# First stage of a one-layer attention kernel: whole-bank casts, projections in sweeps, written order

## The chip, the cores and the metric

The kernel runs on one core of a Trainium2 chip. The metric is device time in microseconds (us); lower is better. A core has a matrix engine (TensorE, PE in the profile; its weight loads are PEld), three engines for elementwise work (VectorE, DVE; ScalarE, ACT; GpSimd, POOL) and a sync engine (SyncE, SP) that issues nearly all DMA transfers here. Each engine runs its own instructions in their order; semaphores order them between engines.

## The reference

One layer with sparse attention (three branches: compressed, selected, window) over x of 512 tokens by 1024. The part that the change touches is the norm, the first two projections and what is made of them:

```python
u = rms_norm(h, pre_norm_gain[layer])
q, kv, g, z = split_cols(h @ w_in, [NSA_WIDTH, 6 * NSA_KV_WIDTH, 3 * H, 3 * NSA_WIDTH])   # h is u here
k_c, v_c, k_s, v_s, k_w, v_w = [a.reshape(B, S, G, dh) for a in jnp.split(kv, 6, axis=-1)]
kc = compress_kv(k_c, k_pos, k_w1, k_w2)
vc = compress_kv(v_c, v_pos, v_w1, v_w2)

def compress_kv(kv, pos, w1, w2):
    idx = jnp.arange(n_cmp)[:, None] * CMP_STRIDE + jnp.arange(CMP_BLOCK)[None, :]
    blocks = kv[:, idx] + pos[None, None, :, None, :]
    ...
    return jax.nn.silu(flat @ w1) @ w2
```

A table of 32 x 16 relative position biases is spread to bias rows for the softmaxes (t5_bucket). The rest (three attentions, gates, output projection, second norm) is the same in both kernels.

## The kernel before, in words

Every float32 product is made of three matmuls on halves of the numbers: a high part (a cast, wh or uh) and a low part (the number less its high part, wl or ul); the products are high x high, low x high, high x low (`pass3`). PSUM has eight banks of 128 x 512 in four pairs, named after what they are for: ps_pj, ps_s, ps_t, ps_o.

The first stage goes through four token tiles of 128. For each, ACT sums the squares (L306), POOL makes r, the inverse root (L86, L90), DVE scales two halves of 512 columns (L316) and PE transposes them, four 128 x 128 blocks into a bank (L321). From the bank ACT casts the high part uh and DVE subtracts for the low part ul, two k tiles, or 256 columns, at a time (L327, L328). Weights come in tiles of 512 rows by 256 columns (wr, one or two DMAs on SP, L103); the cast to wh and the subtraction to wl are ACT's and POOL's for even tiles and DVE's for odd ones (`split_ahead`, L113 to L118).

The k-compressed projection p_kc (tiles 0 and 1, one k half each) runs in two halves of the tokens, matmuls of 256 columns (L247 to L249); the second two token tiles are prepared while the first half runs. Then `tables` spreads the bias table: four matmuls to toep (L344, L345), 16 little ones of 33 x 16 to cb (L351, L352), copies by DVE, and DMAs on SP to DRAM and back (toepd, cmpb, bias, cbs). The v-compressed projection p_vc follows (tiles 2 and 3, matmuls of 512 columns, in two ps_s banks), with DVE's block sums (`blocks`, eight instructions on L407 for k and eight for v) beside it; then the v projection p_v (L480 to L482; tiles 4, 6, 8 and 10 of the weights), between which the compression's own products run (L425 to L427; tiles 5, 7, 9, 11).

The program is given to a scheduler, which sets the order on each engine by its own estimates, except for instructions that are put in written order by `keep_in_program_order`; before, these are only the sums of squares and r. `issue_after(i)` keeps what is written under it behind instruction i.

## Time and profile before

| what | value |
|---|---|
| time, median of 3 runs | 467.64 us (465.06 to 467.78) |
| profiled execution | 466.85 us, its span 465.0 us |
| mean granted clock of PE | 0.993 |
| busy: PE, PEld, DVE, ACT, POOL | 450.9, 375.3, 330.6, 274.3, 184.7 us |
| PE waits in total | 465.0 - 450.9 = 14.1 us |
| first projection matmul, first v-projection matmul | 10.24 us, 41.94 us |

A granted clock of 1.00 is 2.4 GHz and 0.50 is 1.2 GHz. Times within the profile count from the start of the span; the profiled execution's time is 1.85 us over the span. In the rows an entry reads: start, duration, engine, line, operation, out<-in by the program's names, and in brackets the idle time before it with what ended that. Matmuls are pipelined, so two of them overlap: their distance is the difference of their starts.

### The profile page before, as it was taken

What the parts mean: (1) busy time and instruction counts of PE and PEld (TensorE: products, weight loads), DVE (VectorE), ACT (ScalarE), POOL (GpSimd) and SP (SyncE); (2) the same over time, 40 slices, a digit from 0 to 9 for tenths busy, and PEclk for the clock granted to TensorE, in tenths of its full rate; (3) what the DMA queues carried; (4) which work ended last, traced back from release to release, by engine and by line L of the source; (5) the groups of instructions that cost most, each with busy time, mean ns of one, the idle gap of its engine ahead of it and who ended that gap; (6) DMA issues with size and microseconds to landing.
All of it is one profiled execution on the core that took longest, in us unless ns stands there. A gap on an engine that the chain in (4) does not pass through costs nothing.

```text
span 465.0 us, 6924 instructions
## 1 busy us (share of the span) xinstructions
PE 450.9 (97%) x2330; PEld 375.3 (81%) x2330; DVE 330.6 (71%) x801; ACT 274.3 (59%) x642; POOL 184.7 (40%) x185
## 2 busy tenths in 40 slices
PE   5999999999999999999999999999999999999994
PEld 4797888878888878888888788888878888888883
DVE  6869844851766888768769776885896667567685
ACT  5712232542766577767846867666776666467541
POOL 4424544242223453342463525245343342448212
PEclk9989999999999999999999999999999999999998
DMA  8489275263111321511132332024051211214113
GB/s 300 142 82 280 77 216 162 66 206 90 47 45 48 112 59 34 182 45 47 45 90 70 88 94 71 21 57 132 19 180 45 92 45 47 91 43 140 47 45 135
DMA packets 45501, 44.63 MB, mean 96 GB/s; under 512 B 7751, under 2 KB 38471, under 8 KB 45466
## 3 DMA queue, kind: packets, MB, share of 16 engines
q1 hardware_dynamic: 44424, 44.00, 31.9%
q8 instruction: 18, 0.29, 0.3%
q10 hardware_dynamic: 1042, 0.20, 0.2%
q14 instruction: 17, 0.14, 0.1%
HBM read 41.99 MB, written 2.20 MB: 95 GB/s over the span
## 4 chain that ended last, share of the span: by engine, by line
PE 89%; DVE 4%; ACT 3%; issue 2%; POOL 1%; DVEq 0%; POOLq 0%; ACTq 0%
PE ps_pj L146 11%; PE ps_pj L148 11%; PE ps_pj L147 11%; PE ps_s L591 9%; PE ps_t L681 7%; PE ps_o L715 4%; PE ps_o L714 4%; PE ps_pj L834 3%; PE ps_pj L835 3%; PE ps_pj L836 3%; PE ps_s L247 2%; PE ps_s L248 2%; PE ps_s L249 2%; PE ps_pj L247 2%; PE ps_pj L248 1%
## 5 line engine op out<-in xcount | busy, mean ns | idle before, releaser
L118 POOL TENSOR_TENSOR wl<-wr,wh 128x512 fp32r<-128x512 f32 x94 | 123.0, 1328 | 138.6 <-ACT wh L113 122.2
L146 PE MATMUL ps_pj<-uh,wh 128*128 128x512 f32 x240 | 99.0, 412 | 0.0
L148 PE MATMUL ps_pj<-ul,wh 128*128 128x512 f32 x240 | 94.2, 393 | 0.0
L147 PE MATMUL ps_pj<-uh,wl 128*128 128x512 f32 x240 | 94.2, 392 | 0.0
L604 ACT ACTIVATE p<-p,nm 128x512 f32<-128x512 f32 (+3 forms) x128 | 71.6, 560 | 24.3 <-DVE nm L603 23.5
L685 DVE TENSOR_TENSOR ptl<-ps_t,pth 128x512 fp32r<-128x512 f32 x80 | 55.0, 688 | 28.2 <-ACT pth L684 27.7
L113 ACT CAST wh<-wr 128x1024 fp32r<-128x1024 f32 x47 | 49.2, 1047 | 43.5 <-DMA wr<-in_nsa_w_in_dram 20.1
L591 PE MATMUL ps_s<-kd,q 128*128 128x512 f32 (+5 forms) x256 | 63.9, 336 | 0.7 <-DVE zs L699 0.6
L684 ACT CAST pth<-ps_t 128x512 fp32r<-128x512 f32 x80 | 46.4, 580 | 29.3 <-PE ps_t L681 28.7
L148 PEld LDWEIGHTS ps_pj<-ul,wh 128*128 128x128 f32 x240 | 45.1, 188 | 10.1
L591 PEld LDWEIGHTS ps_s<-kd,q 128*128 128x128 f32 x256 | 43.9, 189 | 9.0 <-DVE zs L699 1.2
L146 PEld LDWEIGHTS ps_pj<-uh,wh 128*128 128x128 f32 x240 | 45.2, 188 | 6.1
L147 PEld LDWEIGHTS ps_pj<-uh,wl 128*128 128x128 f32 x240 | 45.3, 189 | 5.8
L603 DVE CUSTOM_DVE_ANT_0 p<-ps_s,bias 128x128 f32<-128x128 f32 (+3 forms) x80 | 34.6, 447 | 20.7 <-PE ps_s L591 20.5
L681 PE MATMUL ps_t<-ident,p 128*128 128x128 f32 x320 | 48.4, 272 | 0.0
L681 PEld LDWEIGHTS ps_t<-ident,p 128*128 128x128 f32 x320 | 39.7, 140 | 9.4
L714 PE MATMUL ps_o<-pth,vt 128*128 128x512 f32 x80 | 33.7, 421 | 0.0
L603 DVE CUSTOM_DVE_ANT_1 p<-ps_s,bias 128x256 f32<-128x256 f32 (+2 forms) x48 | 26.3, 555 | 9.3 <-PE ps_s L591 8.6
L728 POOL TENSOR_TENSOR y<-otmp,zs 128x256 f32<-128x256 f32 x16 | 12.3, 771 | 51.5 <-DVE otmp L725 51.5
L715 PE MATMUL ps_o<-ptl,vt 128*128 128x512 f32 x80 | 32.3, 404 | 0.0
L730 POOL TENSOR_TENSOR otmp<-otmp,zs 128x256 f32<-128x256 f32 x15 | 11.1, 741 | 37.9 <-DVE otmp L725 37.9
L569 ACT ACTIVATE zs<-ps_pj 128x512 f32<-128x512 f32 x22 | 13.1, 596 | 19.4 <-PE ps_pj L148 19.3
(268 smaller groups left out, 895.6 us busy)
## 6 DMA issues: line engine op xcount, KB each, us to landing
wr<-in_nsa_w_in_dram SPq DMA_DIRECT2D x36, 512.0 KB
wr<-in_nsa_w_in_dram SPq DMA_DIRECT2D x16, 256.0 KB
bias<-toepd SPq DMA_DIRECT2D x16, 256.0 KB
wr<-in_nsa_w_out_dram SPq DMA_DIRECT2D x8, 512.0 KB
xt<-in_x_dram SPq DMA_DIRECT2D x4, 512.0 KB
wr<-in_nsa_cmp_k_w_dram SPq DMA_DIRECT2D x4, 512.0 KB
wr<-in_nsa_cmp_v_w_dram SPq DMA_DIRECT2D x4, 512.0 KB
xr<-in_x_dram SPq DMA_DIRECT2D x8, 256.0 KB
```

The costliest lines, as they stand in the source:

```text
L113: A.copy(h[:, 0:kn], raw[:, 0:kn])
L118: el.tensor_tensor(l[:, ks], raw[:, ks], h[:, ks].bitcast(F32), op=ALU.subtract)
L146: T.matmul(p, a, rh, start=k == 0, stop=False)
L147: T.matmul(p, b, rh, start=False, stop=False)
L148: T.matmul(p, a, rl, start=False, stop=k == KT - 1)
L591: T.matmul(po, qs[h][:, qt * 128:(qt + 1) * 128], kds[h // R][:, i, c0:c0 + n], start=i == 0, stop=i == 1)
L603: V.tensor_tensor_reduce(pd, src, bi, 1.0, BIG, ALU.add, ALU.min, st["nm"][:, hh:hh + 1])
L604: A.activation(po, po, AF.Exp, bias=st["nm"][:, hh:hh + 1], scale=-1.0, accum_out=st["rs"][:, hh:hh + 1])
L681: T.transpose(tp[:, hh * 128:(hh + 1) * 128], st["p"][hh][:, c:c + 128], ident)
L685: V.tensor_tensor(pl, tp, ph.bitcast(F32), op=ALU.subtract)
L714: T.matmul(acc, v, ph, start=j == 0, stop=False)
L715: T.matmul(acc, v, pl, start=False, stop=j == qt)
```

## The change

Everything in the first stage is put in written order (`put`). The u tiles are two of [128, 4, 512] for each part instead of four of [128, 2, 512], so that one ACT cast and one DVE subtraction take a whole bank of 512 columns (`high`, `low`). The projections run in sweeps (`sweep`): for one weight tile and one half of the tokens first all eight wh x uh, then eight wh x ul, then eight wl x uh. The v-compressed projection goes to ps_o banks, which two matmuls with a row of zeros open (`open_`); its first k half is swept by token halves among those of p_kc. The sum of squares of tile 2 moves from ACT to DVE (`rms(2, True)`). A third weight tile is loaded and split early. Odd weight tiles are split by ACT and POOL (tiles 1 to 3) or ACT and DVE, where before DVE did both. `load_pos`, the k blocks and `load_w2` are written earlier, `tables` later, behind the sweeps. Buffers with the tag "u" later in the program (y3, og, w3) get the new size.

```diff
-    uh = [keep.tile([128, 2, S], F32R, name=f"uh{i}", tag="u", bufs=8) for i in range(4)]
-    ul = [keep.tile([128, 2, S], F32R, name=f"ul{i}", tag="u", bufs=8) for i in range(4)]
+    uh = [keep.tile([128, 4, S], F32R, name=f"uh{i}", tag="u", bufs=4) for i in range(2)]
+    ul = [keep.tile([128, 4, S], F32R, name=f"ul{i}", tag="u", bufs=4) for i in range(2)]
...
-            tiles.append(split_raw(raws[i], 4, *((V, V) if i % 2 else (A, P))))
+            tiles.append(split_raw(raws[i], 4, *((A, V) if i % 2 and i > 3 else (A, P))))
...
+        zrow = a1.tile([1, 128], F32R, name="zrow")
+        V.memset(zrow.bitcast(F32), 0.0)
...
+        load_ahead(2)
...
-        def rms(t):
...
+        def rms(t, vec=False):
...
+            if vec:
+                put(V.tensor_tensor_reduce(sq, xs[t], xs[t], 1.0 / D, 0.0, ALU.mult, ALU.add, ss))
+            else:
+                put(A.activation(sq, xs[t], AF.Square, scale=1.0 / 32, accum_out=ss))
+            rs_[t] = a1.tile([128, 1], F32, name="r", bufs=4)
+            rstd(rs_[t], ss)
+
+        def scale(t, kq):
+            xt = xs[t][:, kq * 512:(kq + 1) * 512]
+            put(V.scalar_tensor_tensor(xt, xt, rs_[t], gain[kq], op0=ALU.mult, op1=ALU.mult))
+
+        def turn_(t, kq, home):
+            xt = xs[t][:, kq * 512:(kq + 1) * 512]
+            p = pt_[t, kq] = home()
+            for j in range(4):
+                put(T.transpose(p[:, j * 128:(j + 1) * 128], xt[:, j * 128:(j + 1) * 128], ident))
+
+        def norm(t, kq, home):
+            scale(t, kq)
+            turn_(t, kq, home)
...
+        def high(t, kq):
+            put(A.copy(*part(uh, t, kq)))
+
+        def low(t, kq):
+            d, p = part(ul, t, kq)
+            i = put(V.tensor_tensor(d, p, part(uh, t, kq)[0].bitcast(F32), op=ALU.subtract))
+            behind[:] = [i.ins]
+
+        def split_first(n):
+            h = wp.tile([128, 4, 256], F32R, name="wh", tag="wh", bufs=3)
+            l = wp.tile([128, 4, 256], F32R, name="wl", tag="wl", bufs=3)
+            put(A.copy(h, raws[n]))
+            tiles.append((h, l))
+
+            def rest(i):
+                ks = slice(i * 2, i * 2 + 2)
+                put(P.tensor_tensor(l[:, ks], raws[n][:, ks], h[:, ks].bitcast(F32), op=ALU.subtract))
+            return rest
+
+        def open_(ps_):
+            for p in ps_:
+                put(T.matmul(p, zrow, gh[:, 0:S], start=True, stop=False))
+
+        def sweep(n, ps_, kq, hs, opened=False):
+            h, l = tiles[n]
+            for w, u in ((h, uh), (h, ul), (l, uh)):
+                for kk in range(4):
+                    for m, p in enumerate(ps_):
+                        put(T.matmul(p[:, hs], w[:, kk, m * 128:(m + 1) * 128], u[kq][:, kk, hs],
+                                     start=not opened and kq == 0 and w is h and u is uh and kk == 0,
+                                     stop=kq == 1 and w is l and kk == 3))
+                yield
...
+        h0, h1 = slice(0, 256), slice(256, 512)
         rms(0)
         rms(1)
-        prep(0)
-        split_ahead(0)
-        prep(1)
-        split_ahead(1)
-        rms(2)
+        norm(0, 0, tb)
+        high(0, 0)
+        norm(0, 1, tb)
+        w0 = split_first(0)
+        w0(0)
+        w0(1)
+        norm(1, 0, ob)
+        low(0, 0)
+        high(1, 0)
+        norm(1, 1, ob)
+        low(1, 0)
+        p_kc = [pj(), pj()]
+        run(sweep(0, p_kc, 0, h0))
+        high(0, 1)
+        high(1, 1)
+        low(0, 1)
+        low(1, 1)
+        w1 = split_first(1)
+        w1(0)
+        rms(2, True)
+        w1(1)
         rms(3)
-        p_kc = [pj(), pj()]
-        for hh in range(2):
-            hs = slice(hh * 256, (hh + 1) * 256)
-            for k in range(KT):
-                if hh == 0 and k in (3, 5):
-                    prep(2 if k == 3 else 3)
-                h, l = tiles[k // 4]
-                for m in range(2):
-                    ms = slice(m * 128, m * 128 + 128)
-                    pass3(p_kc[m][:, hs], h[:, k % 4, ms], l[:, k % 4, ms], uh[k // 2][:, k % 2, hs],
-                          ul[k // 2][:, k % 2, hs], k == 0, k == KT - 1)
-            if hh == 0:
-                tables()
+        w2 = split_first(2)
+        w2(0)
+        w2(1)
+        s1 = sweep(1, p_kc, 1, h0)
+        next(s1)
+        next(s1)
+        norm(2, 0, tb)
+        high(2, 0)
+        run(s1)
+        norm(2, 1, tb)
+        high(2, 1)
+        scale(3, 0)
+        low(2, 0)
+        low(2, 1)
+        p_vc = [ob(), ob()]
+        open_(p_vc)
+        s2 = sweep(2, p_vc, 0, h0, True)
+        next(s2)
+        turn_(3, 0, tb)
+        high(3, 0)
+        scale(3, 1)
+        next(s2)
+        turn_(3, 1, tb)
+        high(3, 1)
+        low(3, 0)
+        low(3, 1)
+        run(s2)
+        run(sweep(0, p_kc, 0, h1))
+        with tc.issue_after(behind[0]):
+            kpt = load_pos("k")
+            vpt = load_pos("v")
+        run(sweep(1, p_kc, 1, h1))
+        kb = blocks(p_kc, kpt)
+        run(sweep(2, p_vc, 0, h1, True))
+        with tc.issue_after(behind[0]):
+            tables()
...
-        kpt = load_pos("k")
-        vpt = load_pos("v")
-        kb = blocks(p_kc, kpt)
-        p_vc = [sb(), sb()]
-        half_t(2, 0, p_vc)
+        with tc.issue_after(behind[0]):
+            kw2h, kw2l = load_w2("k", 2)
+            vw2h, vw2l = load_w2("v", 1)
+        kb = block_split(kb)
         half_t(3, 1, p_vc)
-        vb = blocks(p_vc, vpt)
-        kw2h, kw2l = load_w2("k", 2)
-        vw2h, vw2l = load_w2("v", 1)
+        vb = block_split(blocks(p_vc, vpt))
...
-                yhl[g] = [keep.tile([128, 2, S], F32R, name=f"y3{i}", tag="u", bufs=8) for i in range(2)]
+                t = keep.tile([128, 2, 2, S], F32R, name="y3", tag="u", bufs=4)
+                yhl[g] = [t[:, i] for i in range(2)]
...
-        og = [keep.tile([128, D], F32, name="og", tag="u", bufs=8) for _ in range(NT)]
+        og = [t[:, i] for t in [keep.tile([128, 2, D], F32, name="og", tag="u", bufs=4) for _ in range(2)] for i in range(2)]
...
-        w3 = [wo_tile(3, 0, [keep.tile([128, 4, 256], F32R, name="w3", tag="u", bufs=8) for _ in range(2)]),
+        wt = keep.tile([128, 2, 4, 256], F32R, name="w3", tag="u", bufs=4)
+        w3 = [wo_tile(3, 0, [wt[:, i] for i in range(2)]),
```

On PE, `tables` moves. Before, its matmuls stand within the first and second token half of p_kc (ps_pj), ahead of most of the second half; uh_80 and uh_81 are high parts, ul_84 a low part.

```order
L321 MATMUL ps_t<-ident,xt 128x128 x4
L344 MATMUL ps_s<-hsr,nth 16x512
L345 MATMUL ps_s<-hsr,ntl 16x512
L247 MATMUL ps_pj<-uh_80,wh 128x256
L321 MATMUL ps_o<-ident,xt 128x128 x4
L344 MATMUL ps_s<-hsr,nth 16x128
L345 MATMUL ps_s<-hsr,ntl 16x128
L248 MATMUL ps_pj<-uh_80,wl 128x256
```

In the changed kernel the same place is this: the last sweep over ps_o (p_vc, tile 2), the matmuls for toep, and then p_vc's second k half with ten matmuls ahead of the first of the 16 little ones (L405, L406).

```order
L379 MATMUL ps_o<-uh_80,wl 128x256 x8
L398 MATMUL ps_s<-hsr,nth 16x512
L399 MATMUL ps_s<-hsr,ntl 16x512
L398 MATMUL ps_s<-hsr,nth 16x128
L399 MATMUL ps_s<-hsr,ntl 16x128
L247 MATMUL ps_o<-uh_81,wh 128x512
L248 MATMUL ps_o<-uh_81,wl 128x512
L249 MATMUL ps_o<-ul_83,wh 128x512
```

The little matmuls moved behind all sweeps, into the projection of 512 columns; 14 of its 24 matmuls follow them.

On DVE, the block sums of k and the copies out of the tables' banks changed places. Before:

```order
L346 COPY toep<-ps_s 16x128
L353 COPY cb<-ps_s 128x8x4x4
L399 TENSOR_TENSOR kw2l<-w2k,kw2h 128x2x64
L398 CAST vw2h<-w2v 128x128
L399 TENSOR_TENSOR vw2l<-w2v,vw2h 128x128
L115 CAST wh<-wr 128x1024
L118 TENSOR_TENSOR wl<-wr,wh 128x512 x2
L463 TENSOR_TENSOR wgs<-wgr,wgs 128x8x48
L390 COPY ptk<-ps_t 128x32
L390 COPY ptv<-ps_t 128x32
L407 TENSOR_TENSOR blk<-ps_pj,ptk 64x16x31 x8
```

Now:

```order
L266 COPY ptk<-ps_t 128x32
L266 COPY ptv<-ps_t 128x32
L274 TENSOR_TENSOR blk<-ps_pj,ptk 64x16x31 x8
L400 COPY toep<-ps_s 16x512
L400 COPY toep<-ps_s 16x128
L118 TENSOR_TENSOR wl<-wr,wh 128x512 x2
L407 COPY cb<-ps_s 128x8x4x4
```

The copies stand behind the eight block sums, and the two wl halves of tile 5 stand between those of toep and that of cb.

On SP the DMAs of the tables stand between other weights. Before (the rows of two 128x2x256 parts are the two halves of tile 4, first, and of tile 6, last; the row named cmp_k_w is tile 5):

```order
L103 DMA wr<-in_nsa_w_in_dram 128x2x256 x2
L103 DMA wr<-in_nsa_cmp_k_w_dram 128x4x256
L347 DMA toepd<-toep 16x640
L356 DMA cmpb<-cb 128x8x4 x4
L163 DMA bias<-toepd 128x512 x4
L168 DMA cbs<-cmpb 128x1x128 x4
L103 DMA wr<-in_nsa_w_in_dram 128x2x256 x2
```

Now (tile 6 in two halves and tile 7 come first; the 128x2x256 part alone ahead of cmpb is the first half of tile 8, the one behind cbs its second half):

```order
L103 DMA wr<-in_nsa_w_in_dram 128x2x256 x2
L103 DMA wr<-in_nsa_cmp_k_w_dram 128x4x256
L401 DMA toepd<-toep 16x640
L103 DMA wr<-in_nsa_w_in_dram 128x2x256
L410 DMA cmpb<-cb 128x8x4 x4
L163 DMA bias<-toepd 128x512 x4
L168 DMA cbs<-cmpb 128x1x128 x4
L103 DMA wr<-in_nsa_w_in_dram 128x2x256
L103 DMA wr<-in_nsa_cmp_k_w_dram 128x4x256
```

The tables' DMAs stood ahead of tile 6 and now stand inside tile 8. From the first matmul of the v projection on, the instructions of PE are the same in the same order to the end.

## Rows read from the trace of the kernel before

**Rows 1.** The page, part 1: busy time, share of the span and instructions.
```profile
PE 450.9 (97%) x2330; PEld 375.3 (81%) x2330; DVE 330.6 (71%) x801; ACT 274.3 (59%) x642; POOL 184.7 (40%) x185
```

**Rows 2.** Waits of PE, whole span: what waited for what, total, times, longest.
```profile
PE ps_o L321 <- DVE xt L316: 0.4, 1, 0.4
PE ps_o L427 <- DVE wl L118: 0.4, 1, 0.4
```

**Rows 3.** Timeline of PE, 6 to 12 us: start, duration, what, idle before.
```profile
6.96 1.12 PE L321 MATMUL ps_t<-ident,xt 128*128 128x128 f32 x4 [1.92 <-DVE xt L316]
...
10.24 0.58 PE L247 MATMUL ps_pj<-uh,wh 128*128 128x256 f32 x1 [0.46 <-ACT uh L327]
...
11.04 0.28 PE L248 MATMUL ps_pj<-uh,wl 128*128 128x256 f32 x1
11.16 0.60 PE L321 MATMUL ps_t<-ident,xt 128*128 128x128 f32 x4
```

**Rows 4.** Timeline of PE, 18 to 29 us.
```profile
19.16 0.63 PE L321 MATMUL ps_t<-ident,xt 128*128 128x128 f32 x4 [0.57 <-issue]
...
24.64 0.58 PE L247 MATMUL ps_pj<-uh,wh 128*128 128x256 f32 x1
...
28.17 0.28 PE L248 MATMUL ps_pj<-uh,wl 128*128 128x256 f32 x1
...
29.00 0.28 PE L249 MATMUL ps_pj<-ul,wh 128*128 128x256 f32 x1
```

**Rows 5.** Busy time by stretch: PE, PEld, DVE, ACT, POOL, PEclk, DMA share, GB/s.
```profile
25.00:28.00 3.00, 3.00 (x15) 3.00 (x15) 1.11 (x5) 0.00 (x0) 0.35 (x1) 0.50 0.89 104
```

**Rows 6.** Timeline of PE, 41 to 58 us.
```profile
41.71 0.39 PE L249 MATMUL ps_s<-ul,wh 128*128 128x512 f32 x1
41.94 0.39 PE L480 MATMUL ps_pj<-wh,uh 128*128 128x512 f32 x1
...
49.63 0.40 PE L480 MATMUL ps_pj<-wh,uh 128*128 128x512 f32 x1
...
56.52 0.40 PE L480 MATMUL ps_pj<-wh,uh 128*128 128x512 f32 x1
```

**Rows 7.** Timeline of SP's DMA queue, 0 to 62 us: start and duration of the issues.
```profile
37.63 1.03 SPq L103 DMA_DIRECT2D wr<-in_nsa_w_in_dram  x2
...
55.70 0.88 SPq L103 DMA_DIRECT2D wr<-in_nsa_w_in_dram  x2
```

**Rows 8.** Timeline of ACT, 36 to 66 us.
```profile
43.46 1.05 ACT L113 CAST wh<-wr 128x1024 fp32r<-128x1024 f32 x1 [4.65 <-DMA wr<-in_nsa_w_in_dram]
...
59.37 1.05 ACT L113 CAST wh<-wr 128x1024 fp32r<-128x1024 f32 x1 [8.47 <-DMA wr<-in_nsa_w_in_dram]
```

**Rows 9.** Timeline of DVE, 0 to 56 us.
```profile
6.15 2.18 DVE L316 SCALAR_TENSOR_TENSOR xt<-xt,r,ps_s 128x512 f32<-128x512 f32 x3 [1.96 <-POOL r L90]
...
24.75 0.29 DVE L353 COPY cb<-ps_s 128x128 f32<-128x128 f32 x1 [1.33 <-PE ps_s L352]
...
28.34 1.29 DVE L118 TENSOR_TENSOR wl<-wr,wh 128x512 fp32r<-128x512 f32 x2
...
31.15 5.49 DVE L407 TENSOR_TENSOR blk<-ps_pj,ptk 64x496 f32<-64x496 f32 x8
...
52.20 3.47 DVE L118 TENSOR_TENSOR wl<-wr,wh 128x512 fp32r<-128x512 f32 x2
```

**Rows 10.** Timeline of POOL, 0 to 66 us.
```profile
8.30 2.50 POOL L118 TENSOR_TENSOR wl<-wr,wh 128x512 fp32r<-128x512 f32 x2 [0.75 <-ACT wh L113]
...
15.10 0.57 POOL L90 TENSOR_TENSOR r<-r,nhalf 128x1 f32<-128x1 f32 x1
...
51.71 3.41 POOL L118 TENSOR_TENSOR wl<-wr,wh 128x512 fp32r<-128x512 f32 x2
```

**Rows 11.** The page, part 5: costliest groups, busy and mean ns, idle before.
```profile
L685 DVE TENSOR_TENSOR ptl<-ps_t,pth 128x512 fp32r<-128x512 f32 x80 | 55.0, 688 | 28.2 <-ACT pth L684 27.7
...
L684 ACT CAST pth<-ps_t 128x512 fp32r<-128x512 f32 x80 | 46.4, 580 | 29.3 <-PE ps_t L681 28.7
```

More of the change, by code (lines that the diff above doesn't have):

```diff
@@ L256, in half_t, with load_pos, blocks @@
                 ms = slice(m * 128, m * 128 + 128)
-                pass3(p, h[:, kk, ms], l[:, kk, ms], uh[k // 2][:, k % 2, :], ul[k // 2][:, k % 2, :],
+                pass3(p, h[:, kk, ms], l[:, kk, ms], uh[k // 4][:, k % 4, :], ul[k // 4][:, k % 4, :],
                       k == 0, k == KT - 1)
+    def load_pos(nm):
+        pr = small[nm, "p"]
+        V.tensor_copy(pr[:, 1], pr[:, 0])
+        p = tb()
+        T.transpose(p[:, :32], pr.rearrange("p a b -> p (a b)"), ident[:32, :32])
+        pt = sm.tile([128, 32], F32, name="pt" + nm)
+        V.tensor_copy(pt, p[:, :32])
+        return pt
+    def blocks(banks, pt):
+        blk = keep.tile([128, 16, G, NCMP], F32, name="blk", tag="kd", bufs=4)
+        for m, p in enumerate(banks):
+            for gp in range(2):
+                for lp in range(2):
+                    V.tensor_tensor(
+                        blk[lp * 64:lp * 64 + 64, :, 2 * m + gp, :],
+                        view(p[gp * 64:gp * 64 + 64, :], lp, [[2, 16], [16, NCMP]]),
+                        view(pt[gp * 64:gp * 64 + 64, :], lp, [[2, 16], [0, NCMP]]), op=ALU.add)
+        return blk
     with tc.tile_pool(name="a1", bufs=1) as a1:
```

55 lines of the change are left out of this document (9 added, 46 removed).

## The prediction

> **What bounds the kernel now.** I read the page's busy shares first: TensorE (PE) is busy for 450.9 of 465.0 us, no other engine for more than 71% [rows 1]. So at most 14.1 us could be won by taking PE's waits away, and nearly all else of a gain has to come from less PE work or a higher clock. The waits of PE come next. About 9 us of the 14.1 lie before the first projection matmul (first rows of [rows 3]): input, norm and transposes, which the change leaves in place. Behind it the first stage has few, such as one of 0.57 us before a transpose [rows 4], one of 0.4 and one of 0.5 on the input chain [rows 2, 3]. Then the clock: in 25 to 28 us the granted clock is 0.50, the 1.2 GHz level [rows 5]. The same row has 15 matmuls of 256 columns in 3.00 us, one in 0.20; afterwards seven distances between such matmuls, 28.17 to 29.00, make 0.83, or 0.119 each [rows 4]. What PE did just ahead of the fall were the 16 little matmuls of the tables, up to 24.64 [rows 4]. From 24.64 to 28.17 stand 16 matmuls, which take 3.53 instead of 16 x 0.119 = 1.90: the low clock costs some 1.6 us.
>
> PE's order is the same in both kernels from the first matmul of the v projection to the end, and so is that of the other engines from about there. So the question is when PE reaches that matmul, which I call T: 41.94 before [rows 6]; and whether something that PE wants later is late.
>
> **The change part by part.** The sum goes by differences to T = 41.94.
>
> *Start of the sweeps, +0.86.* Before, the first projection matmul starts at 10.24 between transposes. Now all 16 transposes of two token tiles stand ahead. The third scaling ends at 6.15 + 2.18 = 8.33 [rows 9]; the first bank is transposed at 6.96 + 1.12 = 8.08 [rows 3]. Its high cast takes 0.58 and its low part 0.69, as the 128x512 forms do that read a bank elsewhere [rows 11]: 8.70 and 9.44. The fourth scaling stands behind that on VectorE (DVE): 9.44 + 0.73 (a third of 2.18) = 10.2; its transposes take some 0.9, as the first bank's do (1.12 with its tail [rows 3]): 11.1 instead of 10.24. Whole-bank casts save ScalarE (ACT) and DVE one fixed cost per pair; both have idle time here, so that is worth nothing on the path. The first three distances of the projection, 10.24 to 11.04, make 0.80 before [rows 3], where at the higher level 3 x 0.119 = 0.36 would do. I take it that this slow start now falls on the transposes: -0.44. If it doesn't, this term is 0.
>
> *PE's work, +0.05.* Four transposes fewer stand behind the start (16 for 20; 0.63 for four [rows 4]): -0.63. Two matmuls that open banks with zeros, 512 columns each at the distance 41.71 to 41.94 of 0.23 [rows 6]: +0.46. Half of the v-compressed projection runs in 48 matmuls of 256 columns at 0.119 instead of 24 of 512 at 0.228: +0.24. All else is only moved.
>
> *Waits that go, -0.98.* The 0.57 and the 0.41 in front of transposes [rows 2, 4] go, as written order leaves 24 matmuls of a sweep between a scaling and the next transpose.
>
> *A wait that comes before token tile 2, +0.13 to +0.98.* The sum of squares of tile 2 moves from ACT to DVE, as one 128x1024 instruction with both inputs in SBUF, at about 12.7; behind it come GpSimd's (POOL) two small steps of r, and these are queued behind a wl half. No row has this instruction. DVE work of that kind beside POOL tensor operations is slow in both: two wl halves on DVE take 1.29 alone (at 28.34 [rows 9]) and 3.47 beside POOL's two, which take 3.41 [rows 9, 10]. With no delay the sum, some 1.3 by these, ends at 14.0, the wl half of 1.25 [rows 10] beside it at 14.4; r's two steps take 0.8 (the second 0.57 [rows 10]), so r is there at 15.2 and the scaled half at 15.95. PE is ready at 11.1 + 40 x 0.119 = 15.86: it loses 0.13 with the handing over. With the wl half waiting for the sum it runs from 14.0 to 15.2, r comes at 16.0, the half at 16.8: 0.98. I take 0.98, because those rows are the nearest. [...]
>
> *The tables, +0.6.* The 16 little matmuls now stand inside the second half of the v-compressed projection, ten matmuls behind the four of toep. They reuse a bank whose copy (toep) stands on DVE behind eight block sums, 5.49 us [rows 9]. These start with the end of the k projection; PE has 24 x 0.119 + 0.6 + 10 x 0.228 = 5.7 us of work meanwhile, and the copies add about 0.9: PE waits some 0.6.
>
> *The low clock, 0, or -1.6 if it stays away.* The same little matmuls follow, now with an idle 0.6 in front. What PE did ahead of the fall is there again, so I count on it: 0. Dense sweeps in front speak for the other end, -1.6.
>
> *T.* 41.94 + 0.86 - 0.44 + 0.05 - 0.98 + 0.98 + 0.6 = 43.0 with both bad ends; 40.6 with both good ones (-0.85, -1.6).
>
> *What follows T: the weights of tile 8, 0 to +2.5.* On the SP queue the tables' DMAs stood ahead of tile 6 and stand now between the two halves of tile 8. Before, from the end of the cb copy, 25.04 [rows 9], it took to 37.63 until the next weights were issued behind cmpb, bias and cbs [rows 7], and these were cast at 43.46, with ACT idle for 4.65 on the DMA [rows 8]: 18.4 after the copy. PE wanted them at 49.63 [rows 6], so nobody saw it. Now PE wants tile 8 at T + 14.6 (56.52 less 41.94 [rows 6]), its low half 0.46 later. The cb copy ends 14 matmuls x 0.228 = 3.2 before T, or 4.8 before it at the low clock. By 18.4 and the casts (1.05 [rows 8], and 1.25 for POOL's first half) the low half is there at T + 17.5, 2.5 late (0.9 with the low clock). By the load of 55.70, cast at 59.37 [rows 7, 8], the time behind the issue is 3.7 and the low half comes at T + 15.4: 0.3 late, or none. Less traffic competes than before, so I take the middle, 1.4, and 0.5 with the low clock.
>
> *Costed at nothing:* the third weight tile loaded early (DMA, long before its sweep), odd tiles' high casts on ACT instead of DVE (ACT idles 4.65 before one of these casts [rows 8]; without that cover 1.05 each), fewer and larger buffers at the end (the same bytes released together), the memset. The wait for a wl of DVE at 91.89, 0.4 [rows 2], may go, as DVE loses work: 0 to -0.4. I take -0.4.
>
> **Sum.** 43.0 - 41.94 = +1.06, +0.5 for tile 8, -0.4: +1.2 with both bad ends. The clock holding gives 1.06 - 1.6 + 1.4 - 0.4 = +0.5 (T = 41.4), and no delay of tile 2 takes 0.85 off either. These four lie from -0.4 to +1.2. I take +0.75, the upper half, since the low clock is likelier than not: 466.85 + 0.75 = 467.6. The profiled execution is 466.85 and the median 467.64 (465.06 to 467.78), 0.8 above it, well within what runs differ by.
>
> **Rivals.**
> *Gain in full.* The clock holds, tile 2 is not delayed, tile 8 lands in time, and the bank copy of toep is early: T = 40.0, -1.9, and 0.4 later: 464.5. For it: all of PE's waits in this stage are small and there are dense sweeps. Against it: the little matmuls are unchanged. Chance 0.2.
> *Tile 8 late.* The mechanism above at its far end: 2.5 of idle PE at about T + 15, and the low clock behind this instead of behind the little matmuls, so with T = 41.4: 466.85 - 0.5 + 2.5 + 1.6 = 470.4. It decides at one point: does the second half of tile 8 land later than T + 12.7 (14.6 + 0.46 - 1.05 - 1.25)? For it: 18.4 us were measured on that chain. Against it: in front of that cast other loads shared the queues, and a normal one takes 3.7. Chance 0.17.
> *A cold first sweep.* The projection's first 24 matmuls run at the 1.2 GHz distance, 3.53/16 = 0.22 [rows 4]: 24 x 0.1 = +2.4 (0.22 less 0.12), so 470.0. Against it: the distance fell to 0.12 by 11.04 to 11.16 after 12 transposes and three matmuls. The Trainium skill ("TensorE: Matmul & The Clock Gate", Part 4: PE-mode transpose) says that transposes do not count as busy in the same way; by that the 16 transposes would not raise the clock, and it is this rival. The rows cannot tell, since matmuls stood there too. Chance 0.08.
>
> **The numbers.** Forecast 467.6, no change, chance 0.55. The range reaches to the full gain and the late tile: 464.2 to 470.5. Under 1% (4.7 us, about what a measurement of this kernel tells from no change) stay all cases one by one; two bad ones together pass +4.7: slower 0.06. Faster by over 1% needs more than every wait and the low clock of this stage: 0.04. Same: 0.90.
>
> **What would show it.** Right: the first sweep at 11.1; T between 40.1 and 43; an idle of 0.6 before the little matmuls, ended by DVE's toep; a clock of 0.50 behind them; behind T the same distances as before but at tile 8. Wrong: r of tile 2 ready before PE is; no low stretch; an idle of over 2 us where tile 8 begins; other waits after 60 us, where I count on an unchanged order.

## The result: slower by half a per cent, for a cause that was named and sized too small

The changed kernel takes 469.02 us (median of 9 runs, 468.38 to 470.96) against 467.03 (9 runs, 465.06 to 467.78) of the kernel before beside it: ratio 1.0054, 95% interval 1.0036 to 1.0072. The forecast was 467.6, no change. The time lies inside the range, but the kernel did get slower, by more than the measurement leaves open, and on the way that stood among the rivals: tile 8 of the weights comes late.

The page's busy shares of the kernel after:

```profile
PE 451.3 (97%) x2356; PEld 375.6 (80%) x2356; DVE 320.7 (69%) x781; ACT 283.1 (61%) x643; POOL 188.6 (40%) x189
```

The profiled execution takes 468.8 us, its span 467.0, 2.0 more than before. PE's busy time is 0.4 longer than in [rows 1], so some 1.6 of the 2.0 are idle time of PE. DVE has lost 9.9, ACT and POOL have gained 8.8 and 3.9. PE's waits (what waited for what, total, times, longest):

```profile
PE ps_pj L554 <- ACT wh L113: 1.9, 1, 1.9
...
PE ps_pj L556 <- POOL wl L118: 0.6, 1, 0.6
...
PE ps_t L516 <- DVE hs L510: 0.3, 1, 0.3
PE ps_o L504 <- DVE wl L118: 0.3, 1, 0.3
```

The first two are new: 1.9 for the high half of a weight tile and 0.6 for its low half. So is the hs wait of 0.3. The wait for a wl of DVE, 0.4 in [rows 2], is still there with 0.3. Where on the way these stand is in PE's timeline (start, duration, what, idle before):

```profile
10.87 1.78 PE L379 MATMUL ps_pj<-uh,wh 128*128 128x256 f32 x8
12.49 1.11 PE L379 MATMUL ps_pj<-ul,wh 128*128 128x256 f32 x8
13.44 1.12 PE L379 MATMUL ps_pj<-uh,wl 128*128 128x256 f32 x8
...
16.70 0.63 PE L342 MATMUL ps_t<-ident,xt 128*128 128x128 f32 x4 [0.22 <-issue]
...
35.64 0.27 PE L405 MATMUL ps_s<-nth,hcr 33*128 33x16 f32 x1
...
37.85 0.40 PE L249 MATMUL ps_o<-ul,wh 128*128 128x512 f32 x1
38.09 0.39 PE L247 MATMUL ps_o<-uh,wh 128*128 128x512 f32 x1
...
40.82 0.39 PE L554 MATMUL ps_pj<-wh,uh 128*128 128x512 f32 x1
...
43.44 0.47 PE L554 MATMUL ps_o<-wh,uh 128*128 128x512 f32 x1 [0.19 <-DVE blk L274]
...
57.04 0.50 PE L554 MATMUL ps_pj<-wh,uh 128*128 128x512 f32 x1 [1.85 <-ACT wh L113]
...
58.40 0.50 PE L556 MATMUL ps_pj<-wl,uh 128*128 128x512 f32 x1 [0.62 <-POOL wl L118]
...
59.20 0.39 PE L556 MATMUL ps_pj<-wl,uh 128*128 128x512 f32 x1
```

Two lines of the kernel before, to be read beside these (its L480 to L482 are L554 to L556 here):

```profile
44.98 0.47 PE L480 MATMUL ps_s<-wh,uh 128*128 128x512 f32 x1 [0.61 <-DVE blk L407]
...
57.67 0.39 PE L482 MATMUL ps_pj<-wl,uh 128*128 128x512 f32 x1
```

Read against [rows 6]: T is 40.82 instead of 41.94, a gain of 1.12. The low stretch of the kernel before, which cost 1.6, is missing here, and that is more than the 1.12. The bank wait behind T (for DVE's block sums) is 0.19 where it was 0.61, so by 45 us PE is 1.49 ahead. The first matmul of tile 8 then stands at 57.04 instead of 56.52, and the third low product of it (59.20 against 57.67 for the same matmul before) is 1.53 behind: tile 8 alone costs 3.0. Behind the little matmuls the distances are 0.23 to 0.24 (37.85 to 38.09), the full clock; the granted clock is 1.00 in every window from 20 to 50 us. From 59 us on the two kernels run at the same pace, but for the hs transpose, which starts at 105.06 instead of 103.09: another 0.44. So -1.12 - 0.37 + 3.02 + 0.44 = +1.97, the 2.0 between the spans.

The chain behind tile 8, first SP's queue (start and duration of the issues), then ACT:

```profile
37.18 0.37 SPq L103 DMA_DIRECT2D wr<-in_nsa_w_in_dram  x1
37.94 3.42 SPq L410 DMA_DIRECT2D cmpb<-cb  x4
41.46 2.59 SPq L163 DMA_DIRECT2D bias<-toepd  x4
46.38 3.40 SPq L168 DMA_DIRECT2D cbs<-cmpb  x4
50.73 0.39 SPq L103 DMA_DIRECT2D wr<-in_nsa_w_in_dram  x1
```
```profile
55.95 1.04 ACT L113 CAST wh<-wr 128x1024 fp32r<-128x1024 f32 x1 [6.77 <-DMA wr<-in_nsa_w_in_dram]
```

The first half of tile 8 is issued at 37.18, the second at 50.73, behind cmpb, four bias loads and cbs. SP stands still from 44.05 to 46.38, since cbs reads what cmpb writes and waits for it to land (waits of SP's queue: total, times, longest):

```profile
SPq L168 <- DMA cmpb<-cb: 3.2, 3, 2.3
```

The queues' shares there (the second last column is the busy share of the DMA engines, the last GB/s):

```profile
42.00:44.00 2.00, 1.81 (x9) 1.21 (x8) 1.95 (x3) 0.60 (x2) 1.73 (x2) 1.00 1.47 12
```

The share of over 1 at only 12 GB/s falls together with cmpb, which is written 4 floats at a time; that the small pieces are the reason is likely, but not shown. After its issue the half tile takes 5.2 until its cast (55.95 - 50.73), where 3.7 was taken from [rows 7, 8].

### The profile page after: what moved, and what is told of

Same layout as the page of the kernel before. It is cut to its first block, busy times and chain, and to the rows that moved or that the text cites. A ratio compares the mean times of both kernels' runs of the same rounds, so it can differ in the third digit from the quotient of the medians.

```text
span 467.0 us, 6979 instructions
## 1 busy us (share of the span) xinstructions
PE 451.3 (97%) x2356; PEld 375.6 (80%) x2356; DVE 320.7 (69%) x781; ACT 283.1 (61%) x643; POOL 188.6 (40%) x189
## 4 chain that ended last, share of the span: by engine, by line
PE 82%; DVE 5%; DMA 4%; ACT 4%; issue 2%; POOL 1%; SPq 1%; DVEq 0%; POOLq 0%; ACTq 0%
PE ps_pj L146 11%; PE ps_pj L147 11%; PE ps_pj L148 11%; PE ps_s L665 8%; PE ps_t L755 7%; PE ps_o L789 4%; PE ps_o L788 4%; DMA bias<-toepd 3%; PE ps_pj L909 3%; PE ps_pj L910 3%; PE ps_pj L911 3%; PE ps_pj L379 3%; PE ps_s L772 1%; PE ps_s L247 1%; PE ps_s L248 1%
## 5 line engine op out<-in xcount | busy, mean ns | idle before, releaser
L118 POOL TENSOR_TENSOR wl<-wr,wh 128x512 fp32r<-128x512 f32 x92 | 119.4, 1318 | 138.4 <-ACT wh L113 115.3
L113 ACT CAST wh<-wr 128x1024 fp32r<-128x1024 f32 x55 | 57.6, 1047 | 47.9 <-DMA wr<-in_nsa_w_in_dram 14.1
L118 DVE TENSOR_TENSOR wl<-wr,wh 128x512 fp32r<-128x512 f32 x18 | 16.6, 956 | 17.0 <-ACT wh L113 12.5
L804 POOL TENSOR_TENSOR otmp<-otmp,zs 128x256 f32<-128x256 f32 x15 | 11.1, 740 | 37.9 <-DVE otmp L799 37.9
```

Of the source, the lines that this page charges most:

```text
L113: A.copy(h[:, 0:kn], raw[:, 0:kn])
L118: el.tensor_tensor(l[:, ks], raw[:, ks], h[:, ks].bitcast(F32), op=ALU.subtract)
```

## Experiments

Theory A: the tables' transfers on SP stand ahead of the second half of tile 8, and that is the loss. Theory B: the loss lies in the restructured stage itself (ACT's casts of odd tiles, the written order), and PE would lose it elsewhere if tile 8 came in time. Theory C: what matters is the low clock behind the little matmuls. Theory D, which came up with e1: once tile 8 is in time, the loads that stand behind the tables' transfers set the pace, cbs first; D2 is the same for the bias loads. Each result is given as the median in us, the number of executions, and the ratio to the kernel before, timed beside it, with its 95% interval. Differences of one matmul's start between two traces are taken from their timelines.

**e1_tile8_first.** Both halves of tile 8 are issued ahead of cmpb, bias and cbs.

```diff
+        load_ahead(8)
+        with tc.issue_after(last_dma[0]):
+            for g in range(G):
+                SP.dma_start(dview(cmpb, ...), cb[:, g])
+            load_bias(0)
...
         vb = block_split(blocks(p_vc, vpt))
```


> The changed kernel with both halves of weight tile 8 issued on SP ahead of the DMAs cmpb, bias and cbs of the tables; all else as it is. Theory A (the loss is the late second half of tile 8, whose DMA stood behind these): its cast comes before 50 us instead of at 55.95, the two waits of PE at 55 to 58.4 us (1.85 and 0.62, with restarts 3.0 in all) go, and the time is 468.8 - 3.0 = 465.8 (465.3 to 466.6). Theory B (the loss lies in the restructured stage itself, in ACT's casts of odd tiles or in written order, and PE would lose it elsewhere): 468 to 469 again, the wait only moved. Tile 9, which now stands behind cbs, is wanted at about 60.5 and should land at about 57: no new wait.

467.28 (12 runs), ratio 1.0003 [0.9989, 1.0017]. The wait is gone. Tiles 7 and 8 are cast one behind the other, tile 8 by 51.22, some 5 us before PE wants it:

```profile
49.22 2.00 ACT L113 CAST wh<-wr 128x1024 fp32r<-128x1024 f32 x2
```

The slowdown against the kernel before is gone with it (ratio 1.0003 after 1.0054). But 1.5 of what A expected (465.8) is missing; B's 468 to 469 did not come either. In this trace the clock falls behind the little matmuls (windows of PE, PEld, DVE, ACT, POOL, clock, DMA share, GB/s, then PE's timeline):

```profile
35.00:40.00 5.00, 4.90 (x27) 4.03 (x26) 3.72 (x7) 2.13 (x4) 1.56 (x2) 0.89 0.55 141
40.00:45.00 5.00, 5.00 (x18) 3.94 (x18) 4.01 (x6) 1.46 (x2) 2.86 (x3) 0.77 1.34 81
```
```profile
38.87 0.61 PE L247 MATMUL ps_o<-uh,wh 128*128 128x512 f32 x1
39.28 0.63 PE L248 MATMUL ps_o<-uh,wl 128*128 128x512 f32 x1
...
42.52 0.39 PE L557 MATMUL ps_pj<-wh,uh 128*128 128x512 f32 x1
```

From 39.28 to 41.84 the distances are 0.43 instead of 0.23, and T is 42.52, 1.7 later than in the changed kernel: the low clock that the prediction counted on came here. It is not the whole answer: the five executions with the lowest mean granted clock (0.992 to 0.995) took 467.1 to 467.5, the other seven (0.997 to 0.999) 466.1 to 467.6, with one median, 467.3. f4 finds what else holds them.

**e4_tile8_behind_cmpb.** As e1, but cmpb stays ahead of the second half; only bias and cbs go behind it.

```diff
             for g in range(G):
                 SP.dma_start(dview(cmpb, ...), cb[:, g])
-            load_bias(0)
...
+        load_ahead(8)
+        with tc.issue_after(last_dma[0]):
+            load_bias(0)
```


> The changed kernel with the second half of tile 8 behind the four cmpb DMAs but ahead of bias and cbs. It is then issued at about 41.4 instead of 50.7. Theory A as a chain on SP (issue after issue): it lands at about 45 to 47, no wait, 465.9. If it is rather the DMA queues that hold it (cmpb's small packets drain slowly, busy engines at 12 to 54 GB/s in 40 to 48 us), it lands later, up to about 50, still in time: the landing time tells them apart, the total does not unless it passes 53.5.

467.12 (12), 1.0003 [0.9988, 1.0017]; no tile 8 wait, the half is issued at 41.19. So the small pieces of cmpb are not enough to make it late; standing behind bias and the waiting cbs is.

**e3_before_tables_in_tile8.** The same order put into the kernel before: the tables' DMAs between the halves of tile 8, nothing else.

```diff
+        with tc.issue_after(SP.dma_start(d0(raw8), s0).ins):
+            for g in range(G):
+                SP.dma_start(dview(cmpb, ...), cb[:, g])
+            load_bias(0)
+        tc.keep_in_program_order(SP.dma_start(d1(raw8), s1))
```


> The kernel before with one part of the change alone: its table DMAs (cmpb, bias, cbs) stand between the two halves of tile 8 on SP instead of ahead of tile 6. Tile 8's first half is issued at about 42.1 there, the second some 12.7 later, lands 5 later: about 60, where PE wants it cast by 56.5. Theory A: PE waits about 4 to 5.5 for it, 471 to 472. Theory B: no change, 466.5 to 467.5, as tile 8 would be covered.

474.34 (6), 1.0151 [1.0124, 1.0178]. The wait has the same name as in the kernel after, 4.5 long, and the clock is low behind it:

```profile
PE ps_pj L487 <- ACT wh L113: 4.5, 1, 4.5
```
```profile
55.00:60.00 5.00, 1.14 (x10) 0.93 (x8) 0.00 (x0) 0.49 (x1) 0.00 (x0) 0.91 1.08 299
60.00:65.00 5.00, 4.26 (x9) 2.96 (x10) 3.70 (x3) 1.60 (x2) 3.87 (x3) 0.50 0.38 130
```

This order alone makes the kernel before slower by more than the whole change does. Here the idle PE is followed by 0.50, as the rival "tile 8 late" had it; behind the shorter waits of the kernel after it is not.

**e2_tables_early.** Another remedy under A: `tables` written one sweep earlier, so that its transfers stand ahead of tile 6 again.

```diff
         run(s2)
+        with tc.issue_after(behind[0]):
+            tables()
         run(sweep(0, p_kc, 0, h1))
```


> The changed kernel with the tables written early, behind the last low part of token tile 3 and ahead of the second token half of the k projection, so that their matmuls stand among 256-column matmuls as in the kernel before and their DMAs ahead of tile 6. Theory A: no wait for tile 8, about 465.8 if the granted clock stays at 1.00 behind the 16 little matmuls. The clock is the second question: if the little matmuls by themselves bring the 0.50 that the kernel before showed in 25 to 28 us, 1.6 more: 467.4; if it was what stood ahead of them there (gaps of PE from 16 to 20 us), none. Theory B: 468 to 469.

471.11 (6), 1.0078 [1.0053, 1.0104]. The tile 8 wait goes, others come, and the clock is 0.88 and 0.78 in 25 to 35 us:

```profile
PE ps_o L554 <- DVE blk L274: 1.2, 1, 1.2
PE ps_t L264 <- PE ps_o L379: 0.9, 1, 0.9
PE ps_s L405 <- DVE toep L400: 0.7, 1, 0.7
```

The wait for tile 8 goes, as A says, but neither A's time (465.8, or 467.4 with the low clock) nor B's came: tables this early interrupt PE at three other places, so the remedy costs more than it gives.

**e5_little_spread** and **e8_before_little_spread.** Theory C's remedy: the little matmuls one by one among large ones, in e1 one behind each of the last sixteen 512-column matmuls, in the kernel before among the second half of the k projection.

```diff
+                for w, u in ((h, uh), (l, uh), (h, ul)):
+                    put(T.matmul(p, w[:, kk, ms], u[1][:, kk, :], start=False, stop=...))
+                    if i > 7:
+                        little(i - 8)
```


> The kernel with tile 8 ahead of the tables' DMAs, and beside that the 16 little matmuls of the tables not in a row but one behind each of the last 16 matmuls of 512 columns of the v-compressed projection. Theory C (the fall to 0.50 follows a stretch in which PE runs only little matmuls): no low stretch in 36 to 46 us, first v matmul at about 40.7 instead of 42.5. Whether that reaches the end is open: POOL finishes the first low half of tile 10 at 63.6 there, just when PE asks for it, since tiles 9 and 10 are issued behind cbs (52.7, 55.2). Theory D (the weights behind the tables' DMAs now set the pace): PE waits about 1.5 for tile 10 and the time stays at 467.0 to 467.4; without D it is 465.7.

> The kernel before with its 16 little matmuls spread between the 256-column ones of the second token half of the k projection, nothing else. Theory C: the granted clock stays at 1.00 there, where it was 0.50 for 25 to 28 us in the profiled execution: -1.6 in executions that had it, so the runs lie at the lower edge of the kernel before, 465.1 to 466.0, median about -1.2. Rival: the fall comes from the gaps of PE at 16 to 20 us, and the runs spread as before, 465 to 468.8, median 467.3.

e5: 474.97 (4), 1.0168 [1.0144, 1.0193]. e8: 470.52 (6), 1.0066 [1.0046, 1.0087]. PE's timeline of e5, then of e8:

```profile
36.07 0.50 PE L537 MATMUL ps_o<-uh,wh 128*128 128x512 f32 x1
36.50 0.27 PE L407 MATMUL ps_s<-ntl,hcr 33*128 33x16 f32 x1
36.71 0.50 PE L537 MATMUL ps_o<-uh,wl 128*128 128x512 f32 x1
```
```profile
25.41 0.27 PE L353 MATMUL ps_s<-ntl,hcr 33*128 33x16 f32 x1
...
26.16 0.27 PE L353 MATMUL ps_s<-nth,hcr 33*128 33x16 f32 x1
```

A pair of one large and one little matmul takes 0.64 (36.07 to 36.71; five such pairs up to 39.23 take 3.16, or 0.63 each), where 0.23 and the 0.11 of little ones in a row make 0.34: a little matmul between large ones costs 0.29 more than one in a row. In e8 three 256-column matmuls and a little one take 0.75 (25.41 to 26.16) for 3 x 0.119 + 0.11 = 0.47: 0.28 more. Why is not shown. e5's clock is low from 39.5 to 53 us besides (0.50 in 40 to 50); e8's stays at 1.00. The remedy costs more than the low clock.

**e6_cbs_behind_tile9**, **e7_odd_tiles_on_dve.** Cbs issued behind tile 9 (e6, on e5); odd tiles from 5 on split by DVE alone (e7, on e6).

```diff
+                with tc.issue_after(last_dma[0]):
+                    load_cbs(0)
...
-            tiles.append(split_raw(raws[i], 4, *((A, V) if i % 2 and i > 3 else (A, P))))
+            tiles.append(split_raw(raws[i], 4, *((V, V) if i % 2 and i > 3 else (A, P))))
```


> As the one with the little matmuls spread, and the four cbs DMAs behind tile 9 on SP instead of ahead of it. Theory D: tile 9 is issued at about 47 instead of 52.7, tile 10 as soon as its buffer is free, about 53.6, and with less in the queues; PE's wait for tile 10 goes or shrinks to under 0.5: 465.7 to 466.3. If the wait for tile 10 comes from its buffer (freed by the low half of tile 7 on DVE) and not from SP's order, it stays at 467.

> As the one with cbs behind tile 9, and the odd weight tiles from 5 on cast by DVE as in the kernel before instead of by ACT. Theory: ACT's casts of odd tiles push the chain to hs at about 103 us, where PE waits 0.3 to 0.5 in the changed kernel and nothing before; that goes, -0.4. Against it: DVE has 0.69 more for each such tile beside the block sums (5.5 us), so a low half of tile 5 or 7 may come late: up to +1.

474.83 (4), 1.0164 and 475.25 (5), 1.0167. The spread little matmuls swamp both; of the times nothing follows. e7's trace has no hs wait any more, e6's still has 0.5, which speaks for ACT's casts as the cause of that wait; g3 below repeats it without the spread.

**f4_cbs_behind_tile9.** e1 with cbs behind tile 9.

```diff
+            if kp == 0:
+                load_ahead(9)
+                with tc.issue_after(last_dma[0]):
+                    load_cbs(0)
```


> The kernel with tile 8 ahead of the tables' DMAs, and the four cbs DMAs behind tile 9 instead of ahead of it; the 16 little matmuls in a row as in the change. Theory D (once tile 8 is in time, the loads behind cbs set the pace: the first low half of tile 10 was done at 63.6, as PE asked for it): tile 9 is issued at about 47 instead of 52.7 and tile 10 some 1 to 2 earlier, and executions in which the clock holds gain up to 1.5: median 466.3 instead of 467.3, lowest 465.3. Without D: the same as with tile 8 first, 467.0 to 467.4.

467.55 (12), 1.0011 [0.9996, 1.0026]. This profile has no low stretch, T is 40.97 and PE 1.2 ahead of the kernel before at 62.4 us, and still the span is 465.3. A second limit shows, tile 10 (waits of PE, ACT's timeline, SP's queue):

```profile
PE ps_pj L563 <- POOL wl L118: 0.7, 1, 0.7
```
```profile
60.97 1.05 ACT L113 CAST wh<-wr 128x1024 fp32r<-128x1024 f32 x1 [3.39 <-DMA wr<-in_nsa_w_in_dram]
```
```profile
53.35 0.96 SPq L163 DMA_DIRECT2D bias<-toepd  x2
54.73 2.09 SPq L103 DMA_DIRECT2D wr<-in_nsa_w_in_dram  x2
```

Tile 10 stands behind the last two bias loads, takes 6.2 to its cast, and with POOL's low half holds PE's lead to 0.4 at 63.5 us; the hs wait takes the rest. e1 and e4 have the same cast at 61.1 and 60.4: with the low clock PE comes later and there is no wait, without it PE waits. So both ways end at the same time, as the executions of e1 do at either clock, and this is why e1, e4 and f4 all measured level with the kernel before.

**f1_eight_little**, **f3_eight_little_square_on_act**, **f2_before_eight_little.** Half as many little matmuls: high and low table side by side as 32 columns, their sum made by DVE (f1, on f4); tile 2's squares back on ACT (f3, on f1); f1's edit in the kernel before (f2).

```diff
-                T.matmul(p[:, j * H:(j + 1) * H], hcr[...], nth, start=True, stop=False)
-                T.matmul(p[:, j * H:(j + 1) * H], hcr[...], ntl, start=False, stop=True)
+                T.matmul(p[:, j * 2 * H:(j + 1) * 2 * H], hcr[...], nt, start=True, stop=True)
...
-        rms(2, True)
+        rms(2)
```


> As the one with cbs behind tile 9, and the tables made by eight matmuls of 32 columns (high and low part of the table side by side, added by DVE) instead of 16 of 16 columns, still in a row. PE's row of little matmuls is 0.95 instead of 1.87: -0.9 by itself. If the length of the row decides on the fall to 0.50 (theory C in its second form: the row, not what stands beside it), the low stretch becomes rare, another -0.8 on the median: 464.8 to 465.5. If the fall comes all the same: 465.4 to 466.4.

> As the one with eight little matmuls, and the sum of squares of token tile 2 on ACT again instead of on DVE. In the changed kernel it kept a low half of POOL for 1.99 instead of 1.25, r was ready at 15.8, and PE idled 0.4 before the transposes of tile 2. ACT does it in 1.25, behind the casts of tile 1's weights, so from about 12.8 to 14.1, as late as DVE, but POOL is not held: r at 15.1, the idle gone, -0.4. If ACT, which then casts the third weight tile 1.2 later, is what PE waits for next, 0 to +0.5.

> The kernel before with eight little matmuls of 32 columns instead of 16 of 16. PE's work falls by 0.9; if the low clock behind them becomes rare as well, by up to 1.6 more in executions that had it. 467.2 - 0.9 = 466.3 if the clock does as before, 465.3 if it holds. If DVE's block sums set when the v projection's bank comes free (PE waited 0.6 for them there), up to half of it is lost again.

f1: 467.06 (12), 0.9999 [0.9982, 1.0017]. PE is 2.1 ahead at 47 us, and 0.35 at 63.5: tile 10, cast at 61.01, takes the gain. f3: 466.69 (12), 0.9986 [0.997, 1.0003]. In 16 to 20 us PE is busy 4.00 of 4, in f1 3.32:

```profile
16.00:20.00 4.00, 4.00 (x32) 3.47 (x31) 2.70 (x6) 2.72 (x5) 3.80 (x5) 1.00 0.67 210
```

Not all of the difference is the square. f1's first eight projection matmuls took 1.04, f3's 1.86, so f1's PE came 0.8 earlier to the wait; T is 39.93 in f1 and 39.91 in f3. f1 and g1 below start alike (1.04 and 1.03), and there tile 2's transposes begin 0.86 behind the last matmul ahead of them with the square on DVE (f1) and 0.16 with it on ACT (g1): 0.7. f3's time is within the noise of f1's, behind the same limit. f2: 466.27 (12), 1.0003 [0.9971, 1.0035]; seven executions took 465.0 to 466.4 with mean granted clocks of 0.996 to 0.999, five took 469.3 to 471.1 with 0.989 to 0.995. Its trace is of one of the seven and has no low stretch, so where and why the five had a lower clock stays open.

**g4_bias_behind_tile11** and **g1_eight_bias_behind_tile11.** The bias loads issued behind tile 11, in f4 (g4) and in f3 (g1).

```diff
-            load_bias(0, False)
...
+            if kp == 1:
+                load_ahead(11)
+                with tc.issue_after(last_dma[0]):
+                    load_bias(0, False)
```


> As the one with cbs behind tile 9, and the four bias DMAs (1 MB) behind tile 11. There tile 10 was issued at 54.7 and cast at 60.97, 6.2 later, with the queues full at 300 to 376 GB/s; a load in empty queues takes 3.7. Theory D2 (tile 10 waits in the queues behind bias): cast by about 58.5, no wait of PE for it, 1.0 of the 1.4 that PE is ahead by then stay: 466.4 in place of 467.5. Rival (its buffer, freed by the low half of tile 7 at 52.6 to 54, sets the time): cast still at 60 to 61, 467.5.

> As the one with eight little matmuls and the square on ACT (466.7, PE 2.15 ahead of the kernel before at 47 us, 0.3 at 64 behind the wait for tile 10), and the bias DMAs behind tile 11. Theory D2: tile 10 is cast by 58.5, PE keeps about 2.1 to 64 us, and the time is 465.0. Rival: 466.7 again.

g4: 467.01 (12), 0.999 [0.9977, 1.0004]; tile 10 is cast at 57.36, no wait for it, but its trace has the low clock again (0.83 in 35 to 45 us), and that takes the lead before tile 10 could. Its five executions with a mean clock of 0.996 or more took 465.7 to 466.2, the other seven 467.0 to 467.4; f4's four with 0.997 or more had taken 466.8 to 467.6. That bears D2 out: with tile 10 in time, a clock that holds reaches the end. g1: 464.72 (5), 0.9946 [0.9932, 0.9961]. Its queue and ACT:

```profile
50.95 0.90 SPq L103 DMA_DIRECT2D wr<-in_nsa_w_in_dram  x2
...
52.48 1.93 SPq L163 DMA_DIRECT2D bias<-toepd  x4
```
```profile
54.83 1.05 ACT L113 CAST wh<-wr 128x1024 fp32r<-128x1024 f32 x1 [1.63 <-DMA wr<-in_nsa_w_in_dram]
```

Tile 10 is cast 6.1 earlier than in f3 (60.92), PE keeps its lead (3.1 at 44 us, 2.6 at 103), and the kernel is faster than the changed one and than the kernel before. Between f3 and g1 only the place of the bias loads differs, and the medians differ by 2.0, so tile 10's place in the queue was the limit. In the traces, though, 0.9 of g1's lead stands ahead of T (38.97 for 39.91), most of it by a quicker start (1.03 for 1.86), which the bias loads don't touch; how much of the 2.0 that makes, the times don't tell. And the eight little matmuls are no part of the change. In the kernel before (f2) they gave a median of 466.27, and of 465.5 in the seven executions with the higher clock. What the mended change is worth by itself is thus some 0.8 to 1.6 of the 2.6 under the kernel before; no run shows it alone.

**g3_tile8_first_odd_on_dve** and **g2_all_together.** Odd tiles from 9 on split by DVE alone, as in the kernel before: in e1 (g3), in g1 (g2).

```diff
-            tiles.append(split_raw(raws[i], 4, *((A, V) if i % 2 and i > 3 else (A, P))))
+            tiles.append(split_raw(raws[i], 4, *((V if i > 8 else A, V) if i % 2 and i > 3 else (A, P))))
```


> The kernel with tile 8 ahead of the tables' DMAs, and the odd tiles from 9 on cast by DVE as in the kernel before instead of by ACT. The wait for hs at about 103 us (0.5, with restart 0.7 against the kernel before) goes: 467.3 - 0.6 = 466.7. Rival (hs is late for another reason): 467.3. DVE's casts may bring back the wait for a wl at 92 us of the kernel before (0.4 against 0.3 now).

> Eight little matmuls, square on ACT, tile 8 and 9 ahead, bias behind tile 11, odd tiles from 9 on cast by DVE. If both places are what took the gain back, PE stays 2.1 ahead of the kernel before to the end: span near 463, 464.6 to 465.2, faster than the kernel before by 0.4 to 0.5%. If one of them is not, 465.2 to 466.

g3: 466.77 (12), 0.9996 [0.9984, 1.0008]; the hs wait, 0.5 in e1, is gone. g2: 464.50 (6), 0.9943 [0.9929, 0.9957], the lowest median measured. It is 2.6 under the kernel before and 4.5 under the changed one. Its step over g1 (0.2) is within the spread of either. Its trace has no hs wait, but PE waits 0.2 for DVE at 68.88, behind DVE's cast of an odd tile (1.46 from 66.68 on), and loses 0.5 of its lead there, about what the hs wait had cost.

## Why the prediction was wrong, point by point

*What failed: "What follows T: the weights of tile 8, 0 to +2.5".* The step had the mechanism, the chain and the two ends right, and took 0.5 (1.4 without the low clock) where the trace shows 3.0. The chain of 18.4 us from the end of the cb copy, read off [rows 7 to 9], is 18.0 in the kernel after: copy to 37.91, cast at 55.95. I took the middle "since less traffic competes than before". That was an argument about bandwidth; most of the 18 us is SP's own order. It issues cmpb for 3.4, bias for 2.6, waits 2.3 for cmpb to land, issues cbs for 3.4, and only then the weights. Its parts differ from trace to trace (cbs takes 5.54 to issue before, 3.40 after), but from the first cmpb to the next weights it is 12.6 in the kernel before (25.07 to 37.63), 12.8 after (37.94 to 50.73) and 12.6 in e3 (41.93 to 54.55). That less traffic would shorten it, no run shows. The rival "tile 8 late" had said where to look: T + 12.7 would be 53.5, the cast stands at 55.95. PE could use the low half at 58.40, T + 17.6, where the far end had T + 17.5: the end that had been measured was right. The 3.0 is more than its 2.5 because PE came to tile 8 another 0.4 earlier through the bank wait behind T (0.61 to 0.19), which the prediction did not list. e3 shows the step alone, e1 its removal.

*"The low clock, 0" (that it comes back).* It did not in the profiled execution of the kernel after (its nine timed ones have mean clocks from 0.989 to 0.999); it did in e1, e2, e4 and g4, which have the same sixteen little matmuls, and not in f4 and g3, which have them too. In e3, where PE's order up to there is that of the kernel before, the windows from 20 to 30 us show 1.00 where before had 0.50 [rows 5]: the same instructions go either way. Of 92 executions of the kernel before that were timed beside the experiments, 48 have a mean clock of 0.992 to 0.994 and a median of 467.6, 44 have 0.995 to 0.997 and 466.3. So about every second one seems to have the low stretch, at a price of 1.3. With eight little matmuls none of five traces (f1, f2, f3, g1, g2) shows it, though five executions of f2 had a lower clock. What tips it with sixteen is open. That it stayed away hid part of the error. The forecast's own sum for a holding clock was +0.5, with T at 41.4; the profile has +2.0. Tile 8 makes 1.6 of that difference, ACT's casts 0.44, the wl wait 0.35, and against them stand 0.6 by the earlier T and 0.4 by the bank wait.

*The start.* Predicted 11.1, is 10.87. The slow start was not saved on the transposes: the first eight matmuls take 1.62, later eights 0.95, so 0.66 are lost against 0.44 before: the term is +0.22, where I had counted -0.44. The cold first sweep did not come: from 12.49 on the distance is 0.119. The granted clock reads 1.00 in 10 to 13 us, although the first distances are about 0.21. Behind the same sixteen transposes the first eight matmuls took 1.03 to 1.07 in five traces (e4, f1, g1, g3, g4) and 1.31 to 1.86 in nine, never a whole sweep, so a quick or slow start is in part luck, and its cause is open. The rule behind that rival (the Trainium skill, "TensorE: Matmul & The Clock Gate", Part 4: PE-mode transpose) says that transposes do not count as busy in the same way. It would fit the nine slow starts, but it does not say why five were quick or why none lasted for a sweep. (About 9 us of waits ahead of the first projection matmul, as I read it, is too much too: PE was busy for 5.15 of the first 10.24, so 5.1 stand there, and 6.2 at the end, behind 440 us.)

*The wait before tile 2, +0.98.* The lock is there (POOL's timeline):

```profile
12.86 1.99 POOL L367 TENSOR_TENSOR wl<-wr,wh 128x512 fp32r<-128x512 f32 x1 [0.65 <-ACT wh L362]
...
15.24 0.57 POOL L90 TENSOR_TENSOR r<-r,nhalf 128x1 f32<-128x1 f32 x1
15.78 1.28 POOL L367 TENSOR_TENSOR wl<-wr,wh 128x512 fp32r<-128x512 f32 x1
```

DVE squares from 12.48 to 13.70; the wl half beside it takes 1.99, the next one 1.28. That is 0.7 of delay, about what remains of the square when the half starts (13.70 - 12.86 = 0.84). By the Trainium skill ("SBUF — State Buffer", Who interferes with whom) a DVE instruction with two SBUF inputs contends with a GpSimd one that reads SBUF, and the second is blocked until the first ends. The trace agrees roughly, with 0.7 of delay for the 0.84 that was left. With the square on ACT the same half takes 1.30 (f3) and 1.29 (g1), and the wait is gone. PE lost only 0.38 (its sweep ended near 16.32, the transpose starts at 16.70), because its own slow start had used up the rest. In f1, which starts quickly, the same transposes begin at 16.68: the chain through r sets their time, and so the terms -0.44 and +0.98 could not be added up as if they were independent.

*The tables, +0.6.* The little matmuls start 0.49 behind the matmul before them (35.15 to 35.64), 0.26 more than a normal distance. In e5 each step from a large to a little matmul has 0.20 of that (36.07 to 36.50, 0.43 for 0.23). The bank copy of toep was nearly in time.

*"Costed at nothing": odd tiles' high casts on ACT.* I gave an idle ACT at one such cast as cover. At 100 us there is none. ACT's timeline of the kernel after:

```profile
99.31 0.59 ACT L203 ACTIVATE q<-ps_pj 64x512 fp32r<-64x512 f32 x1
99.80 1.03 ACT L113 CAST wh<-wr 128x1024 fp32r<-128x1024 f32 x1
100.86 1.21 ACT L203 ACTIVATE q<-ps_pj 64x512 fp32r<-64x512 f32 x2
101.97 0.36 ACT L508 ACTIVATE th<-ps_o 124x256 f32<-124x256 f32 x1
```

th comes after two q and a cast, at 101.97 (99.92 before), hs on DVE behind it, and PE waits 0.3; with the distance behind it 0.44 are lost. g3 takes it away. The 0.4 for the wl wait at 91.89 gave 0.05 (0.36 to 0.31).

So the terms ahead of T were too high: T came at 40.82, 2.2 earlier than the 43.0 of the bad ends, 1.6 of it by the clock, and the bank wait behind it shrank by 0.4. What I had costed behind T was too low, tile 8 by 2.5, ACT's casts by 0.44, the wl wait by 0.35, and that outweighed it. (PE's work, -0.63 + 0.46 + 0.24, is +0.07 and not +0.05, which changes nothing.)

Where the expected gain went: PE is 1.5 ahead at 45 us in the kernel after. Tile 8 takes it. If tile 8 is mended, tile 10 takes what is over 0.4 to 0.8 (f1, f3, f4, g3). Only with both ahead of the bias loads does the lead reach the end (g1, g2); g4 has both ahead too, but in its trace the low clock had taken the lead before. The restructured stage itself won little: without a low stretch T is 40.8 to 41.0 with the change (after, f4, g3) and 41.36 in the order of the kernel before (e3).
